# A two-block fp32 transformer on one core: the closing layer norm on one engine, the last expert pair's halves one after the other, head scaling in another order, two buffers for indexer scores

## The chip, the core and the metric

The kernel runs on one core of a Trainium2 chip. TensorE (PE) multiplies matrices and transposes, VectorE (DVE), ScalarE (ACT) and GpSimd (POOL) work on tiles, and SyncE (SP) issues most DMAs; each engine works through its own queue in order. The metric is the device time of one execution in microseconds (us); lower is better.

## The reference

There are 256 tokens of width 1024. The first block has two layers: token mixing of three branches, layer norm, a mixture of 16 experts with two per token, layer norm. The second block has two layers of RMS norm, an input projection, three kinds of heads (window attention, "fox" attention with a forget gate, mLSTM), an output projection, RMS norm and a two-matrix feed-forward.

```python
def layer_norm(x, g, b):
    ...
    y = (xf - mu) * lax.rsqrt(var + LN_EPS) * g + b

def first_block(x, ...):
    for l in range(DEPTH):
        mix = token_mixing(x, ...)      # pool, indexed attention, memory
        x = layer_norm(DN_ALPHA * x + mix, ln1_g[l], ln1_b[l])
        ffn = moe(x, ...)               # silu(x w1) * (x w3) @ w2, top 2 of 16
        x = layer_norm(DN_ALPHA * x + ffn, ln2_g[l], ln2_b[l])

# indexed attention: which 64 keys a query may use
rel = relu(einsum('bqhd,bsd->bqhs', iq, ik) * IDX_HEAD_DIM ** -0.5)
score = einsum('bqhs,bqh->bqs', rel, iw)
_, sel = lax.top_k(score, n_sel)

# second block, per head
bq = _rms(bq, fox_q_norm); bk = _rms(bk, fox_k_norm)
hc = _rms(mlstm(cq, ck, cv, ci, cf), mlstm_out_norm)
yc = sigmoid(co) * hc
```

## The kernel before

Tokens lie on partitions in two tiles of 128 (b = 0, 1). Dense products run in three fp32r passes (L111 to L113): every weight is split by ACT into a rounded part `wh` (L99, with a gain L104) and by DVE into the rest `wl` (L100, L105); the transposed activations `big` are split the same way after the transposes of L174, by ACT (L176) and DVE (L177). Queues are sorted by the priority of the code that issued an instruction; `tc.high_priority(offset)` moves code ahead, and in the experts' part the order of TensorE is written out by hand.

**Experts.** The 16 experts run as eight pairs, one expert in each half of the partitions. For a pair, `hidden` (L1016) multiplies the gathered tokens by w1 and w3, `turned` (L1027) transposes, `result` (L1037) multiplies by w2 into two PSUM banks, one for each half h of the 1024 columns, four chunks k of the contraction each. Each bank becomes a tile `y` (ACT L1041 the rounded part, DVE L1042 the rest), and `scatter` (L1050) adds both parts of `y` into four banks `acc[2*b+h]`. For the last pair, result's loop takes k outside and h inside, so that both banks end together.

**Closing norm.** `last_norm` (L1112) takes the statistics of the four banks (L1118, in the order b0h0, b1h0, b0h1, b1h1); once b has both halves, `ln_stats` aggregates (DVE L507), adds epsilon (DVE L508) and raises to the power -1/2 on POOL (L509), and `ln_apply` writes the tile `x`: (r - mean) * g by DVE (L518), then for each half either `* rstd + b` by DVE in one instruction (L521, the letter v) or `* rstd` by ACT (L523) and `+ b` by POOL (p) or DVE (a) (L524). Layer 0 uses "aavv" under priority 100, layer 1 "pavv" under none. After layer 1 the transposes of x (L174, 16 of them) open the second block.

**Indexer.** For each b the scores of two heads at a time go to PSUM (L346); ACT rectifies a bank into the tile `rel` (L350, one buffer), and DVE adds each head times its weight to `iacc` (L354). The attention's own scores (L371) use the banks behind them.

**Head norms of the second block.** `head_rstd` squares on ACT (L1198), sums and scales on DVE (L1200, L1201), and takes the power on POOL (L1203). `fox_qk` multiplies q and k by that (L1437) and then by the gain `fg` (L1441); in between, the window attention's softmax rows `sall` are divided on DVE (L1395) for the transposes of L381. `mlstm` multiplies its heads `chn` by the power (L1538) and then by the gate `cgt` (L1540), and TensorE transposes the product (L1543).

Of the kernel before, what the change touches and what calls it, by code (L numbers as in the profile page):

```python
# [7 lines left out]
F32 = mybir.dt.float32  # L8
# [3 lines left out]
AF = mybir.ActivationFunctionType  # L12
# [8 lines left out]
NB = 2  # L21
# [19 lines left out]
class Kernel:  # L41
# [288 lines left out]
    def indexer(self, iqT, ikT, iw, M):  # L330
# [6 lines left out]
        for b in range(NB):  # L337
            n = P * (b + 1)
            acc = self.t(M, [P, S], F32, "iacc", 2)[:, :n]
            per = 512 // n  # L340
            for i0 in range(0, 4, per):
                ps = [self.psa().rearrange("p (h n) -> p h n", h=per) for _ in range(2)]
                for i in range(per):
                    for e in range(2):
                        r = slice(64 * e, 64 * e + 64)
                        nc.tensor.matmul(ps[e][:, i], iqT[r, i0 + i, b * P:b * P + P], ikT[r, :n],  # L346
                                         start=True, stop=True)
                for e in range(2):
                    rel = self.t(M, [P, 512], F32, "rel", 1).rearrange("p (h n) -> p h n", h=per)
                    nc.scalar.activation(rel, ps[e], AF.Relu, scale=0.125)  # L350
                    for i in range(per):
                        h = 2 * (i0 + i) + e
                        prev = cm[:, S - n:] if h == 0 else acc
                        nc.vector.scalar_tensor_tensor(acc, rel[:, i], iw[:, b, h:h + 1], prev,  # L354
                                                       OP.mult, OP.add)
            for _ in range(8):
                m8 = self.t(M, [P, 8], F32, "m8", 2)
                nc.vector.max(m8, acc)
                nc.vector.match_replace(acc, m8, acc, -3.0e38)
            mask = self.t(M, [P, S], F32, f"smask{b}", 1)[:, :n]  # L360
            nc.vector.tensor_scalar(mask, acc, -2.0e38, NEG, OP.is_gt, OP.mult)
            masks.append(mask)
# [146 lines left out]
        nc.gpsimd.tensor_tensor(rs, mv[:, 1:2], self.half, OP.pow)  # L509
        return mv[:, 0:1], rs  # L510

    def ln_apply(self, out, r, ms, g, b, how):


        nc = self.nc
        c = [slice(h * 512, h * 512 + 512) for h in range(2)]
        for h in range(2):
            nc.vector.scalar_tensor_tensor(out[:, c[h]], r[h], ms[0], g[:, c[h]], OP.subtract, OP.mult)  # L518
        for h in range(2):
            if how[h] == "v":  # L520
                nc.vector.scalar_tensor_tensor(out[:, c[h]], out[:, c[h]], ms[1], b[:, c[h]], OP.mult, OP.add)  # L521
            else:
                nc.scalar.activation(out[:, c[h]], out[:, c[h]], AF.Copy, scale=ms[1])  # L523
                (nc.gpsimd if how[h] == "p" else nc.vector).tensor_tensor(  # L524
                    out[:, c[h]], out[:, c[h]], b[:, c[h]], OP.add)

    def ln_rows(self, g, b):

# [392 lines left out]
    def moe(self, l, x, pre):  # L921
# [7 lines left out]
        with tc.tile_pool(name=f"moe{l}", bufs=1, reuse_waits="tile") as E:  # L929
# [98 lines left out]
                nc.scalar.copy(sl, ps)  # L1028
                return sl.rearrange("p (k c) -> p k c", k=4)

            def result(w, hT, gsl, last=False):
                ys = []
                pss = [self.psa() for _ in range(2)]
                for h, k in ([(h, k) for k in range(4) for h in range(2)] if last else
                             [(h, k) for h in range(2) for k in range(4)]):
                    for a in range(2):
                        mm(pss[h][64 * a:64 * a + 64], hT[:, k, 64 * a:64 * a + 64],  # L1037
                           w[k][:, a, h], start=(k == 0), stop=(k == 3))
                for ps in pss:
                    y = self.t(E, [P, 2, 512], F32R, "y", 2)  # L1040
                    nc.scalar.activation(y[:, 0], ps, AF.Copy, scale=gsl)  # L1041
                    nc.vector.scalar_tensor_tensor(y[:, 1], ps, gsl, y[:, 0], OP.mult, OP.subtract)  # L1042
# [33 lines left out]
            for p in range(8):  # L1076
# [23 lines left out]
                if mT is not None:  # L1100
# [4 lines left out]
                last = p, result(w[2], hT, gsl, p == 7), sT  # L1105
            scatter(*last)
            order.__exit__(None, None, None)
        self.R3_.__exit__(None, None, None)
# [3 lines left out]
    def last_norm(self, r, g, b, out, how):  # L1112

        nc = self.nc
        out = self.new_x()
        st = [self.t(self.cp, [P, 2, 6], F32, "bst", 2) for _ in range(NB)]
        for t, h in ((0, 0), (1, 0), (0, 1), (1, 1)):
            nc.vector.bn_stats(st[t][:, h], r[2 * t + h])  # L1118
            if h == 1:
                ms = self.ln_stats(st[t], t)  # L1120
                self.ln_apply(out[:, t], r[2 * t:2 * t + 2], ms, g, b, how[2 * t:2 * t + 2])


    def second_params(self):
# [306 lines left out]
    def fox_qk(self, z, fg, fx, N):  # L1431
        nc = self.nc
        qkT = fx["qkT"] = self.t(N, [P, 4, S], F32, "s4", 4)
        for b in range(NB):
            rs = self.head_rstd(z[:, b, 768:1280], 8, N, "br")
            qk = self.t(N, [P, 512], F32, "row2", 2)
            nc.vector.tensor_tensor(qk.rearrange("p (h d) -> p h d", d=64),  # L1437
                                    z[:, b, 768:1280].rearrange("p (h d) -> p h d", d=64),
                                    rs[:, :, None].to_broadcast([P, 8, 64]), OP.mult)
            q4 = qk.rearrange("p (i h d) -> p i h d", i=2, d=64)  # L1440
            nc.vector.tensor_tensor(q4, q4, fg[:, :, None, :].to_broadcast([P, 2, 4, 64]), OP.mult)  # L1441
            ps = self.psa().rearrange("p (k c) -> p k c", k=4)
            for k in range(4):
                nc.tensor.transpose(ps[:, k], qk[:, k * P:k * P + P], self.ident)
# [36 lines left out]
    def mlstm(self, z, cT, B, og, yh, yl, N):  # L1481
# [7 lines left out]
        for b in range(NB):  # L1489
# [45 lines left out]
            gt = self.t(N, [P, 256], F32, "cgt", 1)  # L1535
            nc.scalar.activation(gt, z[:, b, 2316:2572], AF.Tanh, scale=0.5)
            nc.vector.scalar_tensor_tensor(gt, gt, 1.0, og, OP.add, OP.mult)
            nc.vector.tensor_tensor(hn, hn, rs[:, :, None].to_broadcast(bc), OP.mult)  # L1538
            hf = hn.rearrange("p h d -> p (h d)")
# [104 lines left out]
```

## Time and profile before

| what | value |
|---|---|
| runs | 1623.55, 1620.77, 1624.55 us; median 1623.55 |
| profiled execution, its own time | 1621.03 us |
| its span | 1619.2 us, mean granted clock 0.992 |
| PE busy | 1576.8 us, 97% of the span |
| DVE, ACT, POOL busy | 871.1 (54%), 693.0 (43%), 83.5 us (5%) |
| DMA | 394.70 MB, mean 244 GB/s |

The span is the part of the execution that the trace covers; 1.8 us lie around it. TensorE is busy nearly throughout, so what it waits for, and at which clock it runs, is to be looked at first. The other engines' shares say how much room there is on average, not who is late at a given place.

### The profile page before, as it was taken

The numbers are of one execution on the slowest core, as the hardware profiler recorded it, in microseconds if no ns is written. First come the engines' busy times: TensorE is split into PE (matmuls) and PEld (weight loads), VectorE is DVE, ScalarE is ACT, GpSimd is POOL, SyncE is SP. The second block draws the span as 40 slices with busy tenths as digits, with TensorE's granted clock in tenths as the row PEclk, the third lists the DMA queues.
The fourth block names the chain that finished last, engine by engine and source line by source line (L and its number), as shares of the span: only waits on it lengthen the run. The fifth ranks groups of instructions, "written<-read, shape, count | busy, mean of one in ns | idle before, by whom it ended". The sixth has DMA issues, their size and how long they took to land.

```text
span 1619.2 us, 24826 instructions
## 1 busy us (share of the span) xinstructions
PE 1576.8 (97%) x9844; PEld 1182.7 (73%) x9844; DVE 871.1 (54%) x1818; ACT 693.0 (43%) x1178; POOL 83.5 (5%) x97
## 2 busy tenths in 40 slices
PE   7999999999999999999999998989999999899998
PEld 6888898444446988898444444867988987688897
DVE  5578548311115677657412114786555568765554
ACT  5545644201013544644301013666555565665553
POOL 1000012000000000012000001120000001100000
PEclk9999999999999999999999999999999999999999
DMA  9563697899998653596899997624555554245550
GB/s 314 186 200 107 218 342 256 331 409 409 409 408 309 220 178 117 197 361 240 321 408 409 408 409 277 215 81 130 185 187 188 173 182 131 83 152 191 188 188 33
DMA packets 162558, 394.70 MB, mean 244 GB/s; under 512 B 15716, under 2 KB 21860, under 8 KB 162436
## 3 DMA queue, kind: packets, MB, share of 16 engines
q1 hardware_dynamic: 157184, 384.98, 65.4%
q0 software_dynamic: 2144, 6.91, 1.4%
q8 instruction: 78, 1.28, 0.3%
q10 hardware_dynamic: 3108, 1.16, 0.3%
q14 instruction: 44, 0.36, 0.1%
HBM read 391.97 MB, written 1.05 MB: 243 GB/s over the span
## 4 chain that ended last, share of the span: by engine, by line
PE 44%; DVE 4%; DMA 1%; ACT 1%; POOL 1%; issue 0%; SPq 0%; POOLq 0%; ACTq 0%
PE a L1016 7%; PE d L112 6%; PE d L111 6%; PE d L113 6%; PE a L111 4%; PE a L112 4%; PE a L113 4%; PE a L1037 3%; PE a L956 1%; DMA raw<-in_w_in_dram 1%; DVE wl L105 1%; PE d L1050 1%; DVE sall L1362 1%; PE a L386 1%; PE a L381 0%
## 5 line engine op out<-in xcount | busy, mean ns | idle before, releaser
L100 DVE TENSOR_TENSOR wl<-raw,wh 128x1024 fp32r<-128x1024 f32 (+1 forms) x232 | 284.1, 1226 | 213.5 <-ACT wh L99 210.4
L99 ACT CAST wh<-raw 128x1024 fp32r<-128x1024 f32 (+1 forms) x232 | 240.4, 1038 | 237.0 <-PE d L112 129.2
L111 PE MATMUL d<-big,wh 128*128 128x256 f32 (+1 forms) x976 | 277.4, 285 | 1.5 <-ACT big L176 1.5
L112 PE MATMUL d<-big,wh 128*128 128x256 f32 (+1 forms) x976 | 276.7, 284 | 1.8 <-DVE big L177 1.8
L113 PE MATMUL d<-big,wl 128*128 128x256 f32 (+1 forms) x976 | 276.7, 284 | 0.0
L105 DVE SCALAR_TENSOR_TENSOR wl<-raw,gcols,wh 128x512 fp32r<-128x512 f32 (+1 forms) x224 | 151.7, 712 | 76.8 <-ACT wh L104 76.4
L112 PEld LDWEIGHTS d<-big,wh 128*128 128x128 f32 (+1 forms) x976 | 186.3, 191 | 4.0 <-DVE big L177 2.4
L104 ACT ACTIVATE wh<-raw,gcols 128x512 fp32r<-128x512 f32 (+1 forms) x224 | 143.7, 686 | 105.1 <-PE a L113 38.8
L111 PEld LDWEIGHTS d<-big,wh 128*128 128x128 f32 (+1 forms) x976 | 186.0, 191 | 3.1 <-ACT big L176 2.2
L113 PEld LDWEIGHTS d<-big,wl 128*128 128x128 f32 (+1 forms) x976 | 186.2, 191 | 0.7 <-issue 0.7
L111 PE MATMUL d<-wh,big 128*128 128x512 f32 (+1 forms) x480 | 185.3, 387 | 0.0
L112 PE MATMUL d<-wl,big 128*128 128x512 f32 (+1 forms) x480 | 184.0, 384 | 1.1 <-DVE wl L105 0.9
L113 PE MATMUL d<-wh,big 128*128 128x512 f32 (+1 forms) x480 | 184.4, 384 | 0.2 <-DVE big L177 0.2
L1016 PE MATMUL a<-raw,xg 128*64 128x512 f32 x832 | 182.7, 592 | 0.0
L1016 PEld LDWEIGHTS a<-raw,xg 128*64 128x64 f32 x832 | 59.8, 137 | 118.0 <-issue 109.0
L1021 DVE TENSOR_TENSOR sl<-sl,a 128x512 f32<-128x512 f32 x16 | 11.0, 688 | 188.6 <-PE a L1016 172.3
L1037 PE MATMUL a<-raw,sl 128*64 128x512 f32 x480 | 107.0, 595 | 0.7 <-ACT sl L1028 0.7
L112 PEld LDWEIGHTS d<-wl,big 128*128 128x128 f32 x480 | 90.9, 189 | 17.1 <-DVE wl L105 1.5
L113 PEld LDWEIGHTS d<-wh,big 128*128 128x128 f32 x480 | 90.5, 189 | 17.4 <-issue 1.0
L111 PEld LDWEIGHTS d<-wh,big 128*128 128x128 f32 x480 | 90.8, 189 | 16.9 <-issue 1.3
L111 PE MATMUL a<-wh,s 128*128 128x512 f32 x256 | 101.3, 396 | 0.0
L112 PE MATMUL a<-wl,s 128*128 128x512 f32 x256 | 101.2, 395 | 0.0
(415 smaller groups left out, 2238.8 us busy)
## 6 DMA issues: line engine op xcount, KB each, us to landing
raw<-in_w_dram SPq DMA_DIRECT2D x328, 512.0 KB, 10.2
raw<-in_w_in_dram SPq DMA_DIRECT2D x64, 1024.0 KB, 6.3
raw<-in_w_ff_dram SPq DMA_DIRECT2D x64, 1024.0 KB, 5.4
br<-in_w_dram SPq DMA_DIRECT2D x36, 512.0 KB, 10.2
raw<-in_w_out_dram SPq DMA_DIRECT2D x16, 1024.0 KB, 5.4
raw<-in_w_br_dram SPq DMA_DIRECT2D x12, 1024.0 KB, 5.6
raw<-in_w_mem_kv_dram SPq DMA_DIRECT2D x7, 1024.0 KB, 12.4
gate<-in_w_dram SPq DMA_DIRECT2D x12, 512.0 KB, 10.2
```

The costliest lines, as they stand in the source:

```text
L99: nc.scalar.copy(hi, src)
L100: nc.vector.tensor_tensor(lo, src, hi, OP.subtract)
L104: nc.scalar.activation(hi[:, k], src[:, k], AF.Copy, scale=g)
L105: nc.vector.scalar_tensor_tensor(lo[:, k], src[:, k], g, hi[:, k], OP.mult, OP.subtract)
L111: mm(ps, sh, mh, start=start, stop=False)
L112: mm(ps, sh, ml, start=False, stop=False)
L113: mm(ps, sl, mh, start=False, stop=stop)
L386: nc.tensor.matmul(po[64 * e:64 * e + 64], value(e, k), pT[:, e, k], start=(k == 0), stop=(k == b))
L956: mm(ps[:, kk], part(b, k + kk), s[:, b], start=(i == 0), stop=(i == len(terms) - 1))
L1016: mm(ps[64 * a:64 * a + 64], g_[:, k, 64 * a:64 * a + 64], w[i][k // 2][:, a, k % 2], start=(k == 0), stop=(k == 7))
L1037: mm(pss[h][64 * a:64 * a + 64], hT[:, k, 64 * a:64 * a + 64], w[k][:, a, h], start=(k == 0), stop=(k == 3))
L1050: mm(acc[2 * b + h], sT[:, b * P:b * P + P], ys[h][:, i], start=False, stop=(p == 7 and i == 1))
```

## The change

There are five edits. (1) The tile `rel` gets two buffers. (2) `ln_apply` has DVE do `* rstd + b` for every half in one instruction; ACT's and POOL's steps are gone. (3) `result` takes the halves in turn for the last pair too, and takes its PSUM bank for each half when it comes to it. (4) `last_norm` runs under priority 300. (5) The head scalings multiply by what is known early (fox: the gain, mLSTM: the gate, into a new tile `chf`), and by POOL's power last. Line numbers of the changed kernel are up to seven lower.

```diff
@@ indexer
-                    rel = self.t(M, [P, 512], F32, "rel", 1).rearrange("p (h n) -> p h n", h=per)
+                    rel = self.t(M, [P, 512], F32, "rel", 2).rearrange("p (h n) -> p h n", h=per)
@@ ln_apply
         for h in range(2):
-            if how[h] == "v":
-                nc.vector.scalar_tensor_tensor(out[:, c[h]], out[:, c[h]], ms[1], b[:, c[h]], OP.mult, OP.add)
-            else:
-                nc.scalar.activation(out[:, c[h]], out[:, c[h]], AF.Copy, scale=ms[1])
-                (nc.gpsimd if how[h] == "p" else nc.vector).tensor_tensor(
-                    out[:, c[h]], out[:, c[h]], b[:, c[h]], OP.add)
+            nc.vector.scalar_tensor_tensor(out[:, c[h]], out[:, c[h]], ms[1], b[:, c[h]], OP.mult, OP.add)
@@ result
-                pss = [self.psa() for _ in range(2)]
-                for h, k in ([(h, k) for k in range(4) for h in range(2)] if last else
-                             [(h, k) for h in range(2) for k in range(4)]):
-                    for a in range(2):
-                        mm(pss[h][64 * a:64 * a + 64], hT[:, k, 64 * a:64 * a + 64],
-                           w[k][:, a, h], start=(k == 0), stop=(k == 3))
-                for ps in pss:
+                for h in range(2):
+                    ps = self.psa()
+                    for k in range(4):
+                        for a in range(2):
+                            mm(ps[64 * a:64 * a + 64], hT[:, k, 64 * a:64 * a + 64],
+                               w[k][:, a, h], start=(k == 0), stop=(k == 3))
                     y = self.t(E, [P, 2, 512], F32R, "y", 2)
@@ last_norm
+        with self.tc.high_priority(offset=300):
...
@@ fox_qk
-            nc.vector.tensor_tensor(qk.rearrange("p (h d) -> p h d", d=64),
-                                    z[:, b, 768:1280].rearrange("p (h d) -> p h d", d=64),
-                                    rs[:, :, None].to_broadcast([P, 8, 64]), OP.mult)
-            nc.vector.tensor_tensor(q4, q4, fg[:, :, None, :].to_broadcast([P, 2, 4, 64]), OP.mult)
+            nc.vector.tensor_tensor(q4, z[:, b, 768:1280].rearrange("p (i h d) -> p i h d", i=2, d=64),
+                                    fg[:, :, None, :].to_broadcast([P, 2, 4, 64]), OP.mult)
+            nc.vector.tensor_tensor(q8, q8, rs[:, :, None].to_broadcast([P, 8, 64]), OP.mult)
@@ mlstm
-            nc.vector.tensor_tensor(hn, hn, rs[:, :, None].to_broadcast(bc), OP.mult)
-            nc.vector.tensor_tensor(hf, hf, gt, OP.mult)
+            hf = self.t(N, [P, 256], F32, "chf", 1)
+            nc.vector.tensor_tensor(hf, hn.rearrange("p h d -> p (h d)"), gt, OP.mult)
+            nc.vector.tensor_tensor(h3, h3, rs[:, :, None].to_broadcast(bc), OP.mult)
```

**DVE at the end of the first block**, before, from the last pair's two `y` on (`bst` are statistics, `bmv` mean and variance, `d` the banks):

```order
L1042 SCALAR_TENSOR_TENSOR y_17715<-a_17697,gsl_17681,y_17715 128x512
L1042 SCALAR_TENSOR_TENSOR y_17718<-a_17698,gsl_17681,y_17718 128x512
L1118 BN_STATS bst_17741<-d_11757 128x6
L1118 BN_STATS bst_17742<-d_11759 128x6
L1118 BN_STATS bst_17741<-d_11758 128x6
L1118 BN_STATS bst_17742<-d_11760 128x6
L507 BN_AGGR bmv_17746<-bst_17741 128x2
L105 SCALAR_TENSOR_TENSOR wl_17816<-raw_17809,gcols_17738,wh_17815 128x512
L508 TENSOR_SCALAR bmv_17746<-bmv_17746 128x1
```

The same place now:

```order
L1035 SCALAR_TENSOR_TENSOR y_17704<-a_17695,gsl_17679,y_17704 128x512
L1112 BN_STATS bst_17739<-d_11755 128x6
L1112 BN_STATS bst_17740<-d_11757 128x6
L1035 SCALAR_TENSOR_TENSOR y_17716<-a_17707,gsl_17679,y_17716 128x512
L1144 COPY gcols_17736<-a_17734 128x32
L1112 BN_STATS bst_17739<-d_11756 128x6
L1112 BN_STATS bst_17740<-d_11758 128x6
L507 BN_AGGR bmv_17744<-bst_17739 128x2
L105 SCALAR_TENSOR_TENSOR wl_17812<-raw_17805,gcols_17736,wh_17811 128x512
L508 TENSOR_SCALAR bmv_17744<-bmv_17744 128x1
```

The first two statistics now stand ahead of the second `y`, and the copy `gcols`, which `wl` and ACT's `wh` read, behind it. `wl` still stands between L507 and the epsilon. Behind the rows shown, the tiles of b0 are finished (two L517, two L519) before b1's aggregation; before, L518, L524 and L521 of both were mixed. On TensorE the four `scatter` matmuls of the first half come at once, and the second half's behind them; the 16 transposes still all precede the first dense matmul.

**DVE at fox**, first layer of the second block, before, from the second tile's L1437 on:

```order
L1437 TENSOR_TENSOR row_3941_18822<-z_17776,bry_18820 128x512
L1395 TENSOR_SCALAR sall_3898_18614<-sall_3898_18614,asm_18671 128x128 x2
L1392 TENSOR_TENSOR asm_18727<-asm_18727,ask_18666 128x2
L1441 TENSOR_TENSOR row_3941_18822<-row_3941_18822,fg_17911 128x512
L1393 RECIPROCAL asm_18727<-asm_18727 128x2
L100 TENSOR_TENSOR wl_18974<-raw_18929,wh_18973 128x1024
L1395 TENSOR_SCALAR sall_3905_18642<-sall_3905_18642,asm_18727 128x256 x2
```

The same place now, from the second tile's multiplication by the gain on; the second `brv` (L1195), which POOL's power reads, is three rows ahead of it (before: three rows ahead of L1437):

```order
L1432 TENSOR_TENSOR row_3943_18820<-z_17772,fg_17907 128x512
L1389 TENSOR_SCALAR sall_3900_18612<-sall_3900_18612,asm_18669 128x128 x2
L1386 TENSOR_TENSOR asm_18669<-asm_18669,ask_18636 128x2
L1435 TENSOR_TENSOR row_3943_18820<-row_3943_18820,bry_18818 128x512
L1387 RECIPROCAL asm_18669<-asm_18669 128x2
L1386 TENSOR_TENSOR asm_18725<-asm_18725,ask_18664 128x2
L100 TENSOR_TENSOR wl_18972<-raw_18927,wh_18971 128x1024
L1389 TENSOR_SCALAR sall_3900_18612<-sall_3900_18612,asm_18669 128x128 x2
L1387 RECIPROCAL asm_18725<-asm_18725 128x2
L1386 TENSOR_TENSOR asm_18725<-asm_18725,ask_18664 128x2
L1389 TENSOR_SCALAR sall_3907_18640<-sall_3907_18640,asm_18725 128x256 x2
```

The first tile's multiplication by the gain has moved out of this stretch, to earlier; the weight's `wl` (L100) now stands ahead of the last two divisions of `sall_3900`, the former fourth pair.

**TensorE at the indexer**, first layer, before, from its last score matmuls on (`a_1345` and `a_1346` are the banks of the attention's first scores):

```order
L346 MATMUL a_1304<-ikT_741,t_140_829 128x256 x2
L112 MATMUL d_1637<-big_392,wh_1695 128x256
L113 MATMUL d_1637<-big_391,wl_1696 128x256
L111 MATMUL d_1637<-big_391,wh_1695 128x256
L112 MATMUL d_1637<-big_392,wh_1695 128x256
L113 MATMUL d_1637<-big_391,wl_1696 128x256
L111 MATMUL d_1638<-big_391,wh_1695 128x256
L112 MATMUL d_1638<-big_392,wh_1695 128x256
L113 MATMUL d_1638<-big_391,wl_1696 128x256
L371 MATMUL a_1345<-t_180_1027,t_160_928 128x128 x2
L111 MATMUL d_1638<-big_391,wh_1695 128x256
```

The same place now:

```order
L346 MATMUL a_1304<-ikT_741,t_140_829 128x256
L371 MATMUL a_1345<-t_180_1027,t_160_928 128x128 x2
L112 MATMUL d_1637<-big_392,wh_1695 128x256
L113 MATMUL d_1637<-big_391,wl_1696 128x256
L371 MATMUL a_1346<-t_180_1027,t_160_928 128x128 x2
L111 MATMUL d_1637<-big_391,wh_1695 128x256
```

The second pair of L371 (`a_1346`) stood 18 dense matmuls behind the indexer's last score and now stands two behind it.

## Rows read from the trace of the kernel before

**Rows 1.** What TensorE waited for in all: longest sums (engine, line, releaser, us, times, longest)
```profile
PE a L174 <- POOL x L524: 5.3, 1, 5.3
...
PE a L381 <- DVE sall L1395: 3.9, 6, 0.9
...
PE a L1543 <- DVE chn L1540: 2.2, 3, 0.9
```

**Rows 2.** DVE's timeline, end of the first block (start, length, instruction, count, [idle before])
```profile
991.54 1.59 DVE L1042 SCALAR_TENSOR_TENSOR y<-a,gsl,y 128x512 fp32r<-128x512 f32 x2 [3.34 <-ACT y L1041]
993.05 2.48 DVE L1118 BATCH_NORM_STATS2 bst<-d 128x6 f32<-128x512 f32 x4
...
995.55 0.70 DVE L105 SCALAR_TENSOR_TENSOR wl<-raw,gcols,wh 128x512 fp32r<-128x512 f32 x1
...
999.00 1.04 DVE L524 TENSOR_TENSOR x<-x,gate 128x512 f32<-128x512 f32 x1
...
1000.63 1.40 DVE L521 SCALAR_TENSOR_TENSOR x<-x,brs,gate 128x512 f32<-128x512 f32 x2
```

**Rows 3.** POOL's timeline, the same stretch
```profile
997.87 1.62 POOL L524 TENSOR_TENSOR x<-x,gate 128x512 f32<-128x512 f32 x1 [0.91 <-ACT x L523]
```

**Rows 4.** ACT's timeline, the same stretch
```profile
997.07 1.33 ACT L523 ACTIVATE x<-x,brs 128x512 f32<-128x512 f32 x2 [1.66 <-DVE x L518]
```

**Rows 5.** TensorE's timeline, the same stretch
```profile
992.34 1.91 PE L1050 MATMUL d<-y,selT 128*128 128x512 f32 x7 [0.28 <-DVE y L1042]
999.55 3.91 PE L174 MATMUL a<-ident,x 128*128 128x128 f32 x16 [5.29 <-POOL x L524]
...
1003.68 0.63 PE L112 MATMUL d<-wl,big 128*128 128x512 f32 x1
1004.10 0.63 PE L111 MATMUL d<-wh,big 128*128 128x512 f32 x1
...
1006.30 0.39 PE L111 MATMUL d<-wh,big 128*128 128x512 f32 x1
1006.53 0.39 PE L112 MATMUL d<-wl,big 128*128 128x512 f32 x1
```

**Rows 6.** Windows: length, busy time of PE, PEld, DVE, ACT, POOL, granted clock, DMA
```profile
497.00:501.00 4.00, 4.00 (x11) 3.13 (x12) 2.06 (x2) 0.23 (x1) 0.00 (x0) 0.57 1.02 408
...
999.50:1006.00 6.50, 6.45 (x23) 5.51 (x24) 6.50 (x11) 4.24 (x7) 1.41 (x3) 0.51 0.23 47
```

**Rows 7.** TensorE's timeline ahead of the window at 497
```profile
496.85 0.50 PE L112 MATMUL a<-raw,br 128*128 128x512 f32 x1 [0.95 <-DVE raw L100]
```

**Rows 8.** DVE's timeline, mLSTM of second layer, second half of the tokens
```profile
1372.03 0.42 DVE L1538 TENSOR_TENSOR chn<-chn,cry 128x256 f32<-128x256 f32 x1 [0.90 <-POOL cry L1203]
1372.38 0.68 DVE L1200 TENSOR_REDUCE arv<-junk 128x8 f32<-128x512 f32 x1
1372.97 0.42 DVE L1540 TENSOR_TENSOR chn<-chn,cgt 128x256 f32<-128x256 f32 x1
```

**Rows 9.** One form of the powers on POOL, line L1203: ns least/median/most, first and last start
```profile
L1203 POOL TENSOR_TENSOR ary<-arv,half x4: 1633/1662/2177, 1070.7 to 1375.8; 128x8 f32<-128x8 f32 x4
```

**Rows 10.** DVE's timeline, fox of the first layer
```profile
1089.46 0.69 DVE L1437 TENSOR_TENSOR row<-z,bry 128x512 f32<-128x512 f32 x1 [1.29 <-POOL bry L1203]
...
1091.21 1.20 DVE L100 TENSOR_TENSOR wl<-raw,wh 128x1024 fp32r<-128x1024 f32 x1
```

**Rows 11.** TensorE's timeline, the same stretch
```profile
1090.49 0.43 PE L381 MATMUL a<-ident,sall 128*128 128x128 f32 x2 [0.59 <-DVE sall L1395]
...
1092.82 0.63 PE L381 MATMUL a<-ident,sall 128*128 128x128 f32 x4 [0.94 <-DVE sall L1395]
```

**Rows 12.** TensorE's timeline, indexer of the first layer
```profile
137.99 1.13 PE L346 MATMUL a<-ikT,t 64*128 64x256 f32 x4 [0.57 <-ACT rel L350]
```

**Rows 13.** ACT's timeline, the same stretch
```profile
139.60 0.60 ACT L350 ACTIVATE rel<-a 128x512 f32<-128x512 f32 x1 [1.66 <-DVE iacc L354]
```

**Rows 14.** DVE's weighted sums over the tile rel: ns least/median/most
```profile
L354 DVE SCALAR_TENSOR_TENSOR iacc<-rel,iw,iacc x28: 350/409/479, 136.1 to 640.2; 128x128 f32<-128x128 f32 x14, 128x256 f32<-128x256 f32 x14
```

More of the change, by code (lines that the diff above doesn't have):

```diff
@@ L510, in ln_stats, with ln_apply @@
         return mv[:, 0:1], rs
-    def ln_apply(self, out, r, ms, g, b, how):
+    def ln_apply(self, out, r, ms, g, b):
         nc = self.nc
@@ L1029, in turned, with result @@
                 return sl.rearrange("p (k c) -> p k c", k=4)
-            def result(w, hT, gsl, last=False):
+            def result(w, hT, gsl):
                 ys = []
-                pss = [self.psa() for _ in range(2)]
-                for h, k in ([(h, k) for k in range(4) for h in range(2)] if last else
-                             [(h, k) for h in range(2) for k in range(4)]):
-                    for a in range(2):
-                        mm(pss[h][64 * a:64 * a + 64], hT[:, k, 64 * a:64 * a + 64],
-                           w[k][:, a, h], start=(k == 0), stop=(k == 3))
-                for ps in pss:
+                for h in range(2):
[4 more added lines that the diff above has]
+                               w[k][:, a, h], start=(k == 0), stop=(k == 3))
                     y = self.t(E, [P, 2, 512], F32R, "y", 2)
@@ L1104, in moe @@
                     self.halves = halves
-                last = p, result(w[2], hT, gsl, p == 7), sT
+                last = p, result(w[2], hT, gsl), sT
             scatter(*last)
@@ L1115, in last_norm @@
         out = self.new_x()
[L1116 to L1121, printed above, removed]
+        with self.tc.high_priority(offset=300):
+            st = [self.t(self.cp, [P, 2, 6], F32, "bst", 2) for _ in range(NB)]
+            for t, h in ((0, 0), (1, 0), (0, 1), (1, 1)):
+                nc.vector.bn_stats(st[t][:, h], r[2 * t + h])
+                if h == 1:
+                    ms = self.ln_stats(st[t], t)
+                    self.ln_apply(out[:, t], r[2 * t:2 * t + 2], ms, g, b)
     def second_params(self):
@@ L1436, in fox_qk @@
             qk = self.t(N, [P, 512], F32, "row2", 2)
-            nc.vector.tensor_tensor(qk.rearrange("p (h d) -> p h d", d=64),
-                                    z[:, b, 768:1280].rearrange("p (h d) -> p h d", d=64),
-                                    rs[:, :, None].to_broadcast([P, 8, 64]), OP.mult)
             q4 = qk.rearrange("p (i h d) -> p i h d", i=2, d=64)
-            nc.vector.tensor_tensor(q4, q4, fg[:, :, None, :].to_broadcast([P, 2, 4, 64]), OP.mult)
+            nc.vector.tensor_tensor(q4, z[:, b, 768:1280].rearrange("p (i h d) -> p i h d", i=2, d=64),
+                                    fg[:, :, None, :].to_broadcast([P, 2, 4, 64]), OP.mult)
+            q8 = qk.rearrange("p (h d) -> p h d", d=64)
+            nc.vector.tensor_tensor(q8, q8, rs[:, :, None].to_broadcast([P, 8, 64]), OP.mult)
             ps = self.psa().rearrange("p (k c) -> p k c", k=4)
@@ L1537, in mlstm @@
             nc.vector.scalar_tensor_tensor(gt, gt, 1.0, og, OP.add, OP.mult)
-            nc.vector.tensor_tensor(hn, hn, rs[:, :, None].to_broadcast(bc), OP.mult)
-            hf = hn.rearrange("p h d -> p (h d)")
-            nc.vector.tensor_tensor(hf, hf, gt, OP.mult)
+            hf = self.t(N, [P, 256], F32, "chf", 1)
+            nc.vector.tensor_tensor(hf, hn.rearrange("p h d -> p (h d)"), gt, OP.mult)
+            h3 = hf.rearrange("p (h d) -> p h d", d=64)
+            nc.vector.tensor_tensor(h3, h3, rs[:, :, None].to_broadcast(bc), OP.mult)
             ps = self.psa().rearrange("p (k c) -> p k c", k=4)
```

## The prediction

> **What bounds the kernel now.** I read the table of the engines' shares first: TensorE is busy 97% of the span, so no other engine's saved work counts by itself. Only two things can: time in which TensorE stands still, and time in which it runs at half clock. The sums of TensorE's waits say where the first lies [rows 1]: one pause of 5.3 us ahead of the transposes that open the second block, 3.9 us in six waits for the window attention's divided rows, 2.2 us in three waits for mLSTM's gated heads. The indexer's wait for ACT's rectified scores is .57 in the first layer [rows 12], and the same again in the second. All this is some 12.5 us, 0.8% of the time, and the edits touch each of these places. The windows say where the half clock is: 999.5 to 1006 was granted .51, the lower level of 1.2 GHz, right behind the 5.3 us pause [rows 5, 6].
>
> **Indexer (edit 1): 0.** Before, each rectification waits until DVE has summed the previous tile [rows 13]. With two buffers the second comes at once, which takes away the .57 [rows 12]. But the order shows the second pair of L371 only two dense matmuls behind the scores instead of 18. Its bank is free only when the fourth rectification is done, and that one needs the second tile summed: eight sums of .41 [rows 14], 3.3, behind the first one at about 136, so 139.3, and .60 for itself [rows 13]: 139.9. TensorE gets there at about 139.2 (its scores end at 139.1, .57 earlier now, and the two pairs and two dense matmuls take about .7). So it waits again, about .7, and what was gained is spent. I take 0 for each layer, with -.57 (nothing late) and +.5 (DVE also puts top-k steps between the sums) as bounds.
>
> **First layer's closing norm and last pair (edits 2 to 4): 0.** No wait of TensorE for a closing norm but the one of 5.3 us stands in its sums [rows 1], and that is at the end of the second layer; in the first layer the memory branch's products cover it. The edit swaps an addition by DVE for a DVE instruction of about the same length, .70, half of L521's 1.40 [rows 2], so the cover stays. Were it gone, the cost were at most the same +.9 as below.
>
> **End of the first block (edits 2 to 4): +0.9.** Before, DVE runs the two `y` from 991.54 to 993.13, the four statistics from 993.05 to 995.53, and then without a pause up to the last L521, which ends at 1002.03 [rows 2]. This chain is the pause; ACT's 1.33 and POOL's 1.62 [rows 3, 4] lie beside it. Now the statistics of the first half stand ahead of the second `y`. The first scatter matmuls (.24 apart: seven in 1.91 [rows 5]) land at about 992.1, two statistics (.62 each) bring DVE to 993.35, the second `y` (.80) to 994.15. Then the second half has to be scattered, some .6 in which DVE only copies `gcols`, and two more statistics end at 996.0: half a microsecond later than before. From there DVE needed 6.5 to 1002.03; it now loses L524's 1.04 and gets two instructions of .70, +.36. So x is whole at about 1002.9 instead of 1002.03, +.9. The first transposes start earlier, at about 998.9 (996.0 and .1 + .6 + .1 + 1.3 + .7 of DVE's work, each by its row or its kin in rows 2) instead of 999.55 [rows 5], and the pause shrinks to about 4 us, but all 16 transposes precede the first dense matmul, which therefore moves by the whole +.9.
>
> The bounds: -2.5, if the clock stays up behind the shorter pause. Dense matmuls start .42 apart at the low level (1003.68 and 1004.10) and .23 apart behind it (1006.30 and 1006.53) [rows 5], and some seven ran low, 1.4; the transposes at the end would give another .5, and the earlier start .6. And +2.5, if the low stretch lasts half as long again (stretches differ: 4.0 and 6.5 us in rows 6): 3.2 us more at half speed cost 1.6, on top of .9. I take +.9, since nothing in the rows says that a stretch this thin keeps the clock: at 497 it fell to .57 though the pause just ahead was only .95 [rows 6, 7].
> The Trainium skill ("TensorE: Matmul & The Clock Gate", HAM oscillation) ties the fall to idle gaps of TensorE beyond a length, and says that the phase of the fall varies from run to run; by it alone a pause shortened from 5.3 to 4 could escape now and then, and the sum would be 2 to 2.5 lower. The rows at 497 show that a gap is not needed.
>
> **mLSTM (edit 5): -1.5.** Before, two multiplications follow POOL's power; where DVE has something else between them, that delays TensorE too. In the second layer the power comes in at 1372.03, then .42, a reduction of .68, and another .42 that starts .94 behind the first [rows 8]. After, one multiplication follows. This removes at most the three waits, 2.2 [rows 1]; .3 of the two smaller ones stays, where the gain is one multiplication and what stood between. In the last, TensorE comes .9 earlier to the next wait, which hangs on powers of 1.6 to 2.2 on POOL [rows 9] that move by one multiplication, .42: some .4 is given back. 2.2 - .3 - .4 = 1.5; bounds -2.2 and -.5.
>
> **Fox (edit 5): -1.2, -.6 for each layer.** Before, L1437 holds DVE for 1.29 until POOL's power is in [rows 10], and the divisions queued behind it keep TensorE waiting, .59 and then .94 [rows 11]. After, the gain's multiplication (.69) fills that wait, the first tile's has left the stretch, and the power starts some .9 earlier. But `wl` (1.20 [rows 10]) now stands ahead of the fourth pair of divisions: that pair is later, 1.20 - .9 = .3, and the next ones are right behind it, some 1.4 earlier than before. The waits go from .59 + .94 to about .9 + 0, -.6. Bounds for each layer: -1.5 (both gone) and +.3 (only the delay).
>
> **Sum.** 0 + 0 + .9 - 1.5 - 1.2 = -1.8. Against the profiled execution, 1621.03, this is 1619.2; that one lies 2.5 below the median of the runs, 1623.55, so I put the forecast against the median: **1621.7 us**. The runs before spread over 3.8 us; 0.2%, or 3.2 us, is about what a measurement can tell from no change.
>
> **Rivals.**
> *The gains come in full.* The clock does not fall, or rises with the transposes, and the waits go: -1.0 at the block's end (+.9 - 1.9), -2.0 for mLSTM, -2.2 for fox: -5, 1618.5. For it speaks the shorter pause; against it 497 [rows 7] and the weight in the way at fox. Chance .20.
> *Nothing comes through.* POOL is late next. Its power of 128x8 took 1633 ns at least and 2177 at most [rows 9], and the changed order puts multiplications of two tiles beside it. If each power moved loses .5, fox gives nothing and mLSTM about .9, which the block's end takes back: 0, 1623.5. The Trainium skill ("GPSIMD Engine Reference", Key points) says that POOL shares its SBUF interfaces with DVE and contends with DVE instructions of two SBUF inputs, as these multiplications are; by it this rival would be the rule, and the spread in rows 9 agrees with it in kind. Chance .14.
> *DVE alone is the bound at the block's end, slower.* x comes .9 later, the low clock lasts half as long again (1.6), the indexer's new wait costs .5 in both layers, fox loses .3 twice, and mLSTM gives only .5: .9 + 1.6 + 1.0 + .6 - .5 = +3.6, 1627.2. It decides once the norm's part reaches +2.5 and the head norms give less than .5. Chance .14.
> *The change does not do what it says* in one place: despite its priority, the norm has `wl` between aggregation and epsilon (.70 twice, in the order as before). That is in the sum already.
>
> **How the numbers follow.** The forecast has .52, with a range of its own from 1619 to 1624. Faster by over 0.2% means under 1620.3: nearly all of the first rival, .19, and .15 of the forecast's case: .34. Slower means over 1626.8: most of the last rival, .11. The rest, .55, is within. The range from 1617.5 to 1626.5 leaves out the far part of the first rival (.05) and most of the last (.1).
>
> **What would show it.** Right: with the events ahead of them unmoved, the first transposes of x near 999 but the last L519 near 1003, TensorE waiting on DVE instead of POOL there; low clock behind the pause again; mLSTM's three waits under .6 in all; one wait instead of two around `sall` in each layer; L371 waiting in the indexer. Wrong: a granted clock of 1.0 at the second block's opening, or a first dense matmul earlier than 1003.1; waits at fox unchanged; or two L371 without any wait.

## The result, and the profile after

Slower, where no change was forecast: 1629.1 us (median of six runs, 1626.97 to 1632.29) against 1623.32 us of the kernel before beside it, a ratio of 1.0052 [1.0039, 1.0065]. (The ratios and intervals in this text are those on record. They are not quotients of the medians, which mostly come out lower: here 1.0036, 5.8 us.) The profiled execution took 1626.97 (span 1625.2, mean granted clock .990), the one before 1621.03 (span 1619.2, .992): 5.9 us more.

To see where, I took the start of TensorE's n-th matmul after, minus before, along both traces (the two programs have as many matmuls):

| at (us) | after minus before | what lies ahead of it |
|---|---|---|
| 150 to 250 | +.35 | start of the program, first indexer |
| 302 to 482 | +6.07 | the branch ahead of the first expert block |
| 544 to 615 | +4.4 | before has a half-clock stretch at 497, after none |
| 780 to 960 | +3.8 | second indexer |
| 1030 to 1053 | +4.0 | end of the first block, with its pause |
| 1141 to 1335 | +6.2 | mLSTM and fox of the second block's first layer |
| end | +5.95 | second layer |

Steps of 1 to 2 us can be the clock alone: in the 14 traces of this text the half-clock stretches add up to between 21 and 47 us. The largest step, +5.7, lies at a place that the prediction does not mention. The sums of TensorE's waits of after show it first (engine, line, releaser, us, times, longest):

```profile
PE a L950 <- ACTq L1056: 6.1, 2, 5.6
PE a L174 <- DVE x L519: 5.5, 2, 4.0
...
PE a L1339 <- DVE akk L1335: 3.5, 3, 1.9
PE a L1538 <- DVE chf L1535: 2.5, 4, 1.1
...
PE a L371 <- ACT rel L350: 1.5, 2, 0.8
PE a L381 <- DVE sall L1389: 1.5, 4, 0.7
...
PE d L1043 <- DVE y L1035: 1.2, 1, 1.2
```

Read against [rows 1]: `sall` fell from 3.9 to 1.5, as it should. The pause of 5.3 became two waits, 5.5 in all, `chf` waits 2.5 where `chn` waited 2.2, and `akk` 3.5 where it waited 1.6 before:

```profile
PE a L1345 <- DVE akk L1341: 1.6, 3, 0.8
```

The top line is new in kind. L1056 (L1063 before) is the conditional branch on the experts' overflow; TensorE's gathers (L950) wait there for ACT's sequencer (ACTq). What the branch line shows in the trace (ns least/median/most, first and last start; the first column is the line):

```profile
L1056 ACTq COMPARE_BRANCH  x2: 54/61/68, 285.9 to 782.1; - x2
...
L1056 DVEq EVENT_SEMAPHORE  x2: 21/21/21, 286.4 to 782.6; - x2
L1056 ACTq EVENT_SEMAPHORE  x2: 17/17/17, 290.9 to 782.6; - x2
```

DVE passes from the branch to its next instruction in .5 us; ACT compares at 285.9 and goes on at 290.9. At the second layer's branch (782) both take .5. Before, the same two lines of ACT:

```profile
L1063 ACTq COMPARE_BRANCH  x2: 54/61/68, 286.6 to 778.3; - x2
...
L1063 ACTq EVENT_SEMAPHORE  x2: 17/17/17, 287.2 to 778.7; - x2
```

TensorE's timeline of after behind the branch, and the windows there (columns as in [rows 6]), say what it cost. The wait is 5.55 (before: .94), and a stretch at .54, the lower clock, follows:

```profile
290.92 2.29 PE L950 MATMUL a<-sel,x 128*128 128x128 f32 x9 [5.55 <-ACTq L1056]
```

```profile
285.00:291.00 6.00, 0.45 (x2) 0.08 (x1) 0.36 (x2) 0.07 (x1) 0.00 (x0) 0.90 0.50 198
291.00:297.00 6.00, 6.00 (x30) 6.00 (x31) 0.69 (x1) 1.21 (x1) 0.00 (x0) 0.54 0.00 1
```

So 4.6 of the 5.7 are the wait itself, and about 1 the clock: the records of before have 6.8 us at half clock here (278.8 to 285.7), those of after 3.4 and, behind the branch, 6.8.

The trace lists DMA packets of kind "instruction", but not which engine they are for. In after, four of 8 KB (and one of 16 KB) start between 287.6 and 288.5 and a fifth at 291.4, and ACT goes on at 290.8, behind the four. Before, five such packets start between 287.7 and 288.2, but ACT's next instruction stands at 287.1, ahead of them. The Trainium skill ("Runtime: NRT & Kernel Launch", Instruction fetch mechanics) says that a taken branch whose target is not in the part already fetched has to wait for a DMA of it. The trace fits that, but does not show it: no record tells what ACT did between 286 and 290.8, or whose code the packets held.

Why here and not before? In the traces 318 ACT instructions are recorded ahead of the first branch before, and 319 after: with two `rel` buffers, ACT has one wait instruction more. That is the theory for the first step (A): **one more ACT instruction ahead of the branch shifts ACT's code so that it has to wait there.** Its rival (B) is that the wait comes with `rel`'s data or with other parts of the change, or varies from run to run.

**End of the first block.** TensorE after, and DVE behind the last products (start, length, instruction, count, [idle before]):

```profile
997.90 0.96 PE L1043 MATMUL d<-y,selT 128*128 128x512 f32 x3 [1.17 <-DVE y L1035]
1002.88 1.94 PE L174 MATMUL a<-ident,x 128*128 128x128 f32 x8 [4.01 <-DVE x L519]
1006.31 1.94 PE L174 MATMUL a<-ident,x 128*128 128x128 f32 x8 [1.50 <-DVE x L519]
1007.90 0.77 PE L111 MATMUL d<-wh,big 128*128 128x512 f32 x1
```

```profile
997.11 0.73 DVE L1035 SCALAR_TENSOR_TENSOR y<-a,gsl,y 128x512 fp32r<-128x512 f32 x1
...
998.43 1.30 DVE L1112 BATCH_NORM_STATS2 bst<-d 128x6 f32<-128x512 f32 x2 [0.49 <-PE d L1043]
...
1001.98 1.41 DVE L519 SCALAR_TENSOR_TENSOR x<-x,brs,gate 128x512 f32<-128x512 f32 x2
...
1005.42 1.40 DVE L519 SCALAR_TENSOR_TENSOR x<-x,brs,gate 128x512 f32<-128x512 f32 x2
```

Against [rows 2, 5]: the pause is 4.0, but 1.17 is paid ahead of it and 1.50 in the middle of the transposes, 6.68 in place of .28 + 5.29. The granted clock from 999.7 to 1010 is .50: it fell again, and for longer. But 4.7 us of that stretch lie in the two waits. What TensorE ran at half clock is 5.6 us of work, where before it was 6.3 (999.0 to 1005.9, less .55 of the wait). Along the trace the place costs less than its waits: +.7 from 980 to 1020.

**mLSTM, first layer.** POOL's timeline of after, then of the kernel before:

```profile
1056.18 1.54 POOL L1197 TENSOR_TENSOR cry<-crv,half 128x4 f32<-128x4 f32 x1 [5.41 <-DVE crv L1195]
...
1069.88 0.46 POOL L1168 TENSOR_TENSOR cosk<-k,gk 128x128 f32<-128x128 f32 x1
1070.30 1.49 POOL L1197 TENSOR_TENSOR cry<-crv,half 128x4 f32<-128x4 f32 x1
1073.20 2.07 POOL L1197 TENSOR_TENSOR ary<-arv,half 128x8 f32<-128x8 f32 x1 [1.41 <-DVE arv L1195]
```

```profile
1051.94 1.05 POOL L1203 TENSOR_TENSOR cry<-crv,half 128x4 f32<-128x4 f32 x1 [5.20 <-DVE crv L1201]
...
1066.47 1.04 POOL L1203 TENSOR_TENSOR cry<-crv,half 128x4 f32<-128x4 f32 x1 [1.56 <-DVE crv L1201]
1070.71 1.63 POOL L1203 TENSOR_TENSOR ary<-arv,half 128x8 f32<-128x8 f32 x1 [3.20 <-DVE arv L1201]
```

The power of 128x4 takes half a microsecond longer. DVE's timeline of after says beside what:

```profile
1056.06 0.75 DVE L105 SCALAR_TENSOR_TENSOR wl<-raw,gcols,wh 128x512 fp32r<-128x512 f32 x1
1057.75 0.43 DVE L1535 TENSOR_TENSOR chf<-chf,cry 128x256 f32<-128x256 f32 x1 [0.94 <-POOL cry L1197]
...
1069.86 1.03 DVE L105 SCALAR_TENSOR_TENSOR wl<-raw,gcols,wh 128x512 fp32r<-128x512 f32 x1
1071.82 0.43 DVE L1535 TENSOR_TENSOR chf<-chf,cry 128x256 f32<-128x256 f32 x1 [0.94 <-POOL cry L1197]
```

Each time DVE is already inside an L105, which reads two tiles (`raw` and `wh`), when the power starts. Before, the L105 beside the first power started at 1052.03, behind the power's start, and the power took 1.05. All 14 traces agree: 52 powers start inside an L100 or L105, and each takes longer by the rest of that instruction less .14 (.44 for a rest of .59, .91 for 1.05). By these figures the power is not slowed but held until DVE's instruction is nearly over. A power does not hold DVE in turn: an L105 that starts while a power runs takes .74 to .75, as usual (42 of them). The one at 1069.86 took 1.03, with `cosk` (128x128) beside it. TensorE's waits in this layer were .76, .75 and .34, and are .50, 1.15 and 1.87 (for `akk`, behind the longer `ary`): +1.7 of the +2.2 in the table. Theory A here is that the new order alone does this; B is that it hangs on the changes ahead of it. In the second layer the same waits shrink by .5: .50, .33, 1.04 and .63 in place of .51, .89, 1.10 and .49. A wait for `cden` beside them grows from .22 to .64 and takes nearly all of that back.

### The profile page after: what moved, and what is told of

It reads as the page before. It is cut to its first block, busy times and chain, and to the rows that moved or that the text cites. A ratio compares the mean times of both kernels' runs of the same rounds, so it can differ in the third digit from the quotient of the medians.

```text
span 1625.2 us, 24830 instructions
## 1 busy us (share of the span) xinstructions
PE 1577.7 (97%) x9844; PEld 1185.8 (73%) x9844; DVE 870.7 (54%) x1819; ACT 692.1 (43%) x1174; POOL 81.7 (5%) x96
## 3 DMA queue, kind: packets, MB, share of 16 engines
HBM read 391.97 MB, written 1.05 MB: 242 GB/s over the span
## 5 line engine op out<-in xcount | busy, mean ns | idle before, releaser
L100 DVE TENSOR_TENSOR wl<-raw,wh 128x1024 fp32r<-128x1024 f32 (+1 forms) x232 | 284.1, 1226 | 214.1 <-ACT wh L99 210.8
L105 DVE SCALAR_TENSOR_TENSOR wl<-raw,gcols,wh 128x512 fp32r<-128x512 f32 (+1 forms) x224 | 151.7, 712 | 75.6 <-ACT wh L104 75.2
```

The lines of the kernel that those rows point to most:

```text
L100: nc.vector.tensor_tensor(lo, src, hi, OP.subtract)
L105: nc.vector.scalar_tensor_tensor(lo[:, k], src[:, k], g, hi[:, k], OP.mult, OP.subtract)
```

## The experiments

All ratios are to the kernel before on the same chip (medians of 1620.28, 1620.51 and 1620.73 us). In each expectation A is the reading that stands ahead of it here, and B the rival to it.

**Edit 1 alone** (`rel_alone`), and **all but edit 1** (`without_rel`):

```diff
-                    rel = self.t(M, [P, 512], F32, "rel", 1)...
+                    rel = self.t(M, [P, 512], F32, "rel", 2)...
```

> The kernel before with the second buffer for rel alone. In the trace of the changed kernel TensorE stands 5.55 us ahead of the first layer's gather, because ACT, after its branch at the experts' overflow test, goes on only 4.8 us later (.4 before); ACT's queue holds one instruction more ahead of that branch than before (319 recorded, 318 before). Theory A (place of the code): the extra instruction comes from this edit and moves the branch and its target against the blocks in which ACT's code is loaded; then this kernel shows the same wait of 5 to 6 us and is 4 to 5 us slower than before, since the indexer gives back .45 in each layer. Theory B (the wait comes from another edit, or by chance of a run): the wait is about .9 here, and the kernel .9 us faster than before.

> The changed kernel with one buffer for rel, all other edits kept. Theory A: ACT's branch is again where it was before, the wait is about .9, and the kernel is 4 to 5 us faster than the changed one: 1623 to 1625.5 us, about the kernel before plus the 2 us that the trace shows lost around the window attention of the second block's first layer. Theory B: the wait of 5 to 6 us stays, and the time is 1629 to 1630.

`rel_alone`: 1626.99 us, 1.0046 [1.0032, 1.0059]. `without_rel`: 1622.82, 1.0019 [1.0010, 1.0028]. The waits at the branch, first of `rel_alone`, then of `without_rel`:

```profile
PE a L956 <- ACTq L1063: 5.1, 2, 4.4
```

```profile
PE a L950 <- DVEq L1056: 1.0, 1, 1.0
PE a L950 <- ACTq L1056: 0.6, 1, 0.6
```

One digit in a buffer count costs nearly all of the change's loss, and the wait goes and comes with it. That excludes the other parts of the change, not yet `rel`'s data.

**One instruction that has nothing to do with the indexer** (`pad1`), and **forty** (`pad40`): the kernel before, with a copy of one column by ACT at the program's start; in `pad40` the last line stands in a loop of 40.

```diff
+        pad = self.cp.tile([P, 1], F32, name="pad")
+        nc.scalar.copy(pad, self.ident[:, 0:1])
```

> The kernel before with one tiny copy (128 x 1) on ACT's queue at the start of the program and nothing else; its result is not used. Theory A: the branch moves by one instruction as in the changed kernel, TensorE waits 5 to 6 us ahead of the first layer's gather, and the time grows by 5 to 6 us, 1628 to 1630. Theory B (it is the indexer's edit as such, or chance): no change, wait .9, 1622 to 1625.

> The kernel before with 40 such copies at the start, some 8 us of ACT's time at a place where TensorE waits for DMA. Theory A says that the wait depends on where the branch falls among the blocks of code, so 40 instructions further on the long wait should be gone again or be of another length: a wait of about 1 us if the target is loaded with the branch, and a time of 1622 to 1630 with the start's own cost of 0 to 6. If every shift gives the long wait, it is not the place among blocks but the distance from the start.

`pad1`: 1624.81, 1.0029 [1.0017, 1.0040]; `pad40`: 1616.23, .9979 [.9968, .9990]. The branch, first of `pad1`, then of `pad40`:

```profile
PE a L958 <- ACTq L1065: 4.2, 2, 3.5
```

```profile
PE a L959 <- DVEq L1066: 1.5, 1, 1.5
PE a L959 <- ACTq L1066: 0.7, 1, 0.7
```

It is shown that the number of ACT's instructions ahead of the branch decides: one more brings the wait, forty more take it away. From ACT's comparison to its next instruction it is 4.79, 3.73 and 2.81 in the three traces with 319 recorded ahead (after, `rel_alone`, `pad1`), and .40 to .41 in the eleven others of this text, with 318 (eight traces), 358 (`pad40`) and 359 (`after_pad40`, `best`). TensorE's wait is 3.5 to 5.6 in the three and .8 to 1.5 in the eleven, so it is neither chance nor `rel`'s data. Why 319 is the bad number is not shown. The time of `pad1` lies below A's 1628 to 1630, and that of `pad40` below its 1622 to 1630. I had not expected `pad40` to be faster than before; its new tile moves most other tiles by 32 bytes, so I tried that alone.

**The unused tile alone** (`place_alone`):

```diff
+        self.cp.tile([P, 1], F32, name="pad")
```

> The kernel before with an unused tile of 128 x 1 among the constants; no instruction is added, but most tiles lie 32 bytes further on. In the runs with padding copies, which need that tile too, the feed-forward's 256-column matmuls start 116.7 ns apart, in all other runs 119.8 ns. Theory A (it is the tiles' place): 116.7 ns here too, and the kernel 3 to 6 us faster than before, with ACT's branch unmoved. Theory B (it is the copies or the run): 119.8 ns and no change. This also says how much of pad1 and pad40 is the branch alone.

1616.04, .9976 [.9965, .9986]: the whole gain of `pad40`, with no instruction changed and no long wait at the branch (.84). The first and last of 19 matmuls in a row, before, then with the tile:

```profile
1140.79 0.28 PE L111 MATMUL d<-big,wh 128*128 128x256 f32 x1
...
1142.95 0.28 PE L111 MATMUL d<-big,wh 128*128 128x256 f32 x1
```

```profile
1140.82 0.28 PE L113 MATMUL d<-big,wl 128*128 128x256 f32 x1
...
1142.93 0.28 PE L113 MATMUL d<-big,wl 128*128 128x256 f32 x1
```

That is 2.16 us for 18 steps against 2.11. Along the trace the gain builds up evenly in the second block's long runs of these matmuls (from -.4 at 1119 us to -2.6 at 1309, from -2.6 at 1446 to -4.4 at 1569), where the starts are 119.9 ns apart before and 116.7 to 116.9 here. In all nine traces without the tile they are 119.8 to 119.9, and in all five with it 116.7 to 117.0. In the first block the same form keeps 119.8 with the tile too. Which tile's place matters was not tried. It also means that `pad1` holds this gain: against `place_alone`, the lone copy costs 1.0029/.9976 = 1.0053, more than `rel_alone`. Its profile has another 13.7 us at half clock at 635. That is not the chance of one run alone: its eleven runs had a mean granted clock of .989, those of `place_alone` .9925. Why the copy should lower it stays open. The runs of after had .989 and those of `rel_alone` .990, the kernel before .993, so some half clock goes with the wait.

**The norm alone**, edits 2 to 4 (`norm_alone`):

```diff
-            if how[h] == "v":
...
+            nc.vector.scalar_tensor_tensor(out[:, c[h]], out[:, c[h]], ms[1], b[:, c[h]], OP.mult, OP.add)
...
-            def result(w, hT, gsl, last=False):
+            def result(w, hT, gsl):
...
+        with self.tc.high_priority(offset=300):
```

> The kernel before with the closing norm by DVE alone, under priority 300, and the last pair's halves in turn (edits 2 to 4). Theory A: in the second layer x is whole .5 to 1 us later than before, seen from the last expert products, TensorE's waits there grow from 5.6 us to 6 to 7, nothing changes in the first layer, and the kernel is .3 to 1.5 us slower, more if the low clock lasts longer. Theory B (shorter chain): TensorE's waits there shrink and the kernel is 1 us or more faster.

1621.32, 1.0004 [.9992, 1.0015]. The waits are those of after:

```profile
PE a L174 <- DVE x L519: 5.3, 2, 3.8
...
PE d L1043 <- DVE y L1035: 1.2, 1, 1.2
```

5.3 + 1.2 against 5.3 + .3: +.9. Along the trace it is +.3 (980 to 1020), as part of the half clock falls into the second wait. The size is below what the runs resolve, and they do not contradict it.

**Edit 5 in its two halves** (`mlstm_alone` and `fox_alone`, each with the lines of the change's diff under that name), **both** (`heads`), and **both in the second layer only** (`heads_late`); the last with the old and the new lines under a flag that is set for the second layer:

```diff
+            if self.late:
...
+            else:
...
```

> The kernel before with only mLSTM's multiplications exchanged (gate first, power last). The order on POOL shows two of the rope rows (sink) moved ahead of cosk and so directly ahead of the second power cry, as in the changed kernel, where cry took 1.54 and 1.49 us in the first layer (1.05 before) and the wait for akk grew from .75 to 1.9. Theory A (the loss of 2.2 us between 1062 and 1141 is this edit's): the same waits, and the kernel 1 to 2 us slower than before. Theory B (as predicted): 1.5 us faster, and the loss belongs to fox or to the norm's shift.

> The kernel before with only fox's multiplications exchanged (gain first, power last). ACT's branch stays where it was. In the changed kernel the waits for the divided rows fell from 3.9 us in six to 1.5 in four. Theory A (fox's part was right, and the losses come from elsewhere): the waits for the divided rows are 1.5 to 2 us, and the kernel is .5 to 2 us faster than before. Theory B (the gain's multiplication only moves the wait to TensorE's earlier scores or to POOL): within .5 us of before, with the waits spread over other lines.

> The kernel before with both head norms exchanged (fox and mLSTM), nothing else. Fox alone lost 5.5 us, most of it in a stretch of 10 us at half clock behind the softmax of the second block's first layer, where its order left TensorE no dense matmuls between the transposes; the changed kernel's trace has no such stretch. Theory A (the low clock there comes from fox's order alone, and mLSTM's edit changes that order back): no low stretch of over 4 us between 1080 and 1105, and the kernel 2 to 3.5 us slower than before, by mLSTM's later powers. Theory B (the losses add): 6 to 9 us slower.

> The kernel before with both head norms exchanged in the second block's second layer only. Theory A (the exchange itself helps; the loss in the first layer comes from POOL's rope rows and a weight's split beside the powers, which the second layer does not have): TensorE's waits for mLSTM's heads in the second layer fall from 1.4 to about .8, those around the divided rows from 2.0 to about 1, and the kernel is .5 to 1.5 us faster than before. Theory B (the exchange brings nothing where it is not disturbed): within .4 us of before.

| kernel | us | ratio |
|---|---|---|
| `mlstm_alone` | 1622.48 | 1.0021 [1.0009, 1.0033] |
| `fox_alone` | 1626.01 | 1.0042 [1.0027, 1.0058] |
| `heads` | 1622.06 | 1.0012 [1.0001, 1.0022] |
| `heads_late` | 1619.15 | .9995 [.9987, 1.0004] |

`mlstm_alone` has the powers of after, so the order alone makes them, and A's 1 to 2 us holds by the medians (2.0):

```profile
1064.39 1.49 POOL L1203 TENSOR_TENSOR cry<-crv,half 128x4 f32<-128x4 f32 x1
1067.29 2.06 POOL L1203 TENSOR_TENSOR ary<-arv,half 128x8 f32<-128x8 f32 x1 [1.41 <-DVE arv L1201]
```

`fox_alone` went as neither theory had it. The windows of its first layer:

```profile
1078.00:1083.70 5.70, 5.70 (x32) 4.15 (x30) 5.70 (x40) 3.12 (x10) 2.36 (x2) 1.00 0.05 12
1083.70:1087.10 3.40, 1.61 (x9) 0.68 (x8) 2.08 (x16) 3.40 (x15) 1.86 (x2) 1.00 0.00 0
1087.10:1097.40 10.30, 9.45 (x41) 5.89 (x42) 6.84 (x25) 6.48 (x20) 0.07 (x1) 0.50 0.01 2
```

With fox's edit alone, the order puts the dense matmuls ahead of the softmax, and for 3.4 us TensorE is busy only 1.61 (three waits, none over .92). Then 10.3 us run at half clock, which at half speed is about 5 us: most of its loss. All six of its runs had a mean clock of .988 to .991, the kernel before .993, so it is not the chance of one run. (Stretches of 3.4 us stand at this place in four other traces, with the old order there.) In `heads` there is none, as A has it (its time, 1.3 slower by the medians, is below A's 2 to 3.5), and fox's waits (`sall`) are small, as forecast:

```profile
PE a L1345 <- DVE akk L1341: 3.6, 3, 1.9
PE a L1544 <- DVE chf L1541: 2.5, 4, 1.2
PE a L381 <- DVE sall L1395: 1.5, 4, 0.6
```

By the ratios fox's half gives back about half of what mLSTM's half costs, at best (1.0012 against 1.0021; the intervals overlap). The traces do not show it: in the first layer (1050 to 1141) `heads` loses 2.2 us and `mlstm_alone` 2.2 too. `heads` is 1.2 ahead of that at 1119, and then loses 1.1 by 1127, of which .3 is a longer wait for `big` and the rest was not traced. Kept to the second layer (`heads_late`), the edit costs nothing, and its gain is within the noise, so A and B stay undecided there: the waits for the divided rows fell from 3.9 us to 2.5 in all, but those for `akk` grew from 1.6 to 2.8.

**After without the branch's wait** (`after_pad40`: the changed kernel with the forty copies), and **the best of it** (`best`: before with edit 1, the forty copies and their tile):

> The changed kernel with the 40 copies of pad40 at the start, so that ACT's branch falls where pad40 had it, and most tiles 32 bytes further on. Theory A (of the changed kernel's loss, most is the late ACT branch, some 2 to 3 us are the head norms, and the tiles' place is worth 4.5): the wait ahead of the first gather is about 1 us, and the time is 1617 to 1620 where the kernel before has 1620.5: not slower than before. Theory B (the long wait belongs to the edits themselves): it stays at 5 us, and the time is 1623 to 1626.

> The kernel before with two buffers for rel, the 40 copies (which keep ACT's branch away from the bad place, and move the tiles by 32 bytes): what the runs point to as better than both. Theory A: the indexer gives .45 in each layer on top of pad40's gain, 1614.5 to 1616 where the kernel before has 1620.5, 4.5 to 6 us faster. Theory B (the indexer's gain is lost later in the layer): as pad40, 4 us faster.

`after_pad40`: 1619.38, .9992 [.9979, 1.0005]: the loss is gone. Its two parts agree: .0019 of `without_rel` less the tile's .0024 makes -.0005, measured -.0008. `best`: 1615.86, .9981 [.9969, .9992]. It beats both kernels, as `pad40` and `place_alone` do, and is no better than these. Its indexer gains .4 in each layer along the trace, too little to show in the time, so its A and B cannot be told apart.

## Why the prediction was wrong, step by step

**The step that failed is "Indexer (edit 1): 0".** The edit was costed at its two waits in the indexer alone ("I take 0 for each layer, with -.57 ... and +.5 ... as bounds"). That it adds one ACT instruction ahead of the branch was put at nothing without being looked at. In its place the runs showed a wait of 5.55 in place of .94, and +5.7 along the trace with the clock behind it. The order of ACT's instructions would have shown one wait more, but not its price: no row of before shows such a stall. It cost .46% alone, the change .52%. The parts: .46 + .12 (`heads`) + .04 (`norm_alone`) = .62%, inside the interval of the whole (.39 to .65). By the medians they are .41 + .08 + .05 = .54% against .36%, so the sum is no finer than .2%.

**Indexer: nearly right.** The waits at L346 for `rel` went (1.1), and one at L371 came in each layer, 1.5 in the two, as worked out (.7 each). The net along the trace was -.4 in each layer rather than 0, so something beside the waits gained .6; that was not traced.

**First layer's norm: right.** No new wait of TensorE there.

**End of the block: right in the waits.** +.9 forecast, +.9 in the waits of `norm_alone`, +1.1 in after; the first transposes and the last L519 stand where the signs had them (999.1 and 1003.0, less the 3.8 that lie ahead). Not foreseen was the second wait of 1.5 in the middle of the transposes. The half clock lasted longer in after (10.3 us in place of 6.8), but 4.7 us of that lay in the waits, so the bound of +2.5 was not reached. The other bound, -2.5, was too wide from the start: it counts the earlier transposes (.6) as a gain, though the dense matmul behind them moves by +.9, and the first rival has -1.0 for the same case.

**mLSTM: wrong in sign, -1.5.** The sum priced POOL's powers as before, and had them only move by one multiplication. In the first layer they take 1.5 for 1.05 and 2.07 for 1.63, since they now start beside an L105, and `sink` and `cosk` stand right ahead of the second one. Measured alone it is +.21%, 2.0 us by the medians; its trace loses 2.2 in the first layer and gains .4 in the second, up to 1390. This was the mechanism of "Nothing comes through", which lost .5 for each power moved; I held it to .14 and let it give 0 at worst.

The sentence on rows 9 was nearer the truth than the sum. Their spread is this contention: the power of 2177 starts inside an L105 with .69 to go, and takes .54 more than the least. The Trainium skill ("GPSIMD Engine Reference", Key points) names such contention; this case shows which of the two waits, and how long.

**Fox: right in the waits, wrong in the sum, -1.2.** 3.9 became 1.5, but beside mLSTM's edit the first layer's trace is no shorter for it, and alone it lost 5.5 us, most of it by the clock. The sum took the waits that it removes for time gained and looked at no place behind them.

**The slower rival was right in sign and wrong in cause:** it put the loss at the block's end, in the indexer and at fox.

**Clock.** I held that a stretch can lose the clock without a long gap [rows 6, 7]. `fox_alone` is a stronger case than the row at 497. In the four traces with the shorter pause ahead of the transposes (3.8 to 4.0: after, `without_rel`, `norm_alone`, `after_pad40`) the clock fell each time, for 6.8 to 10.3 us.

## What to carry to other kernels

Where a program has a branch, look at each engine's way through it in the trace (its comparison and its next instruction), in every version: a stall of 3 to 5 us can come with one instruction more ahead of it, and a change that is measured beside it has to be measured with the stall shifted away. For a step that waits for POOL, add the rest of the DVE instruction inside which it will now start; its mean hides that. And before a gain of .2% is put down to an edit, run a kernel that only moves the tiles: here an unused tile gained more than any of the edits.

## What was not expected of the hardware

- ACT's way through this branch: .40 to .41 us with 318, 358 or 359 recorded instructions ahead of it, 2.8 to 4.8 with 319.
- POOL's power, started inside an L100 or L105, is held for the rest of it less .14: 128x4 1.54 us in place of 1.05, 128x8 2.07 in place of 1.63.
- A tile that nobody uses, which moves most others by 32 bytes, made the second block's 256-column matmuls start 116.7 to 117.0 ns apart in place of 119.8, and the kernel .24% faster [.14, .35].
- TensorE's clock halved for 10.3 us behind 3.4 us in which it was busy 1.61, with no wait over .92.
